# Decoder layer on one core: the down projection in two column passes, with every third chunk of two row tiles as seven block products

## The chip, the cores and the metric

The kernel runs on one core of one Trainium2 chip. The metric is the time of one execution on the device in microseconds (us), as the median of several runs. The core has five engines that run their own queues in order: TensorE (PE, with PEld for the loading of its stationary operand), VectorE (DVE), ScalarE (ACT), GpSimd (POOL) and SyncE (SP, which here only issues DMA transfers).

## The reference, cut to what matters

One decoder layer, 256 tokens of 2048 features: a combined projection, two kinds of attention, an output projection and a layer norm, and then the part that the change is about:

```python
def conv_ffn(h, w_up, conv_w, conv_b, w_down):
    u = h @ w_up
    g, val = u[..., :FFN_DIM], u[..., FFN_DIM:]
    ...
    gc = conv_b + sum(conv_w[j] * gp[:, j:j + S] for j in range(CONV_W))
    return (jax.nn.silu(gc) * val) @ w_down
...
f = conv_ffn(h, w_up[l], conv_w[l], conv_b[l], w_down[l])
h = layer_norm(DEEPNORM_ALPHA * h + f, ln2_g[l], ln2_b[l])
```

FFN_DIM is 5632, so the down projection multiplies [256 tokens, 5632] by [5632, 2048], all float32.

## The kernel before, in words

**Products in three parts.** TensorE is fed float32r operands. Each float32 operand is split into hi (rounded by a ScalarE copy) and lo (the VectorE difference between the operand and hi), and a product is the sum of hi\*hi, hi\*lo and lo\*hi. So each weight chunk costs ScalarE one pass (L122, in `split`) and VectorE one pass (L123), each in two halves of 128x1024; each tile of activations costs one pass of 128x256 on either engine (L447 and L448, in `split_act`).

**A stream of chunks.** All weights come as one stream of chunks of 1 MB, [128 rows, 2048 columns], the raw chunks in 4 buffers (`raws`) and the hi and lo halves in 6 buffers each (`splits`). A step of the program works off one chunk. The order of the instructions on every engine is the order in which the program is written out; nothing reorders it. At the start of step i, `begin(i)` issues what runs ahead: the split of the activations of chunk i+2, the second half of the split of chunk i+2, the DMA of chunk i+6 on SP, and then whatever an earlier step left to be done now (`at`, `pending`). Halfway through, `middle(i)` issues the first half of the split of chunk i+3. As the engines work their queues in order, an instruction that waits for a buffer holds back all that was issued after it on its engine.

**The down projection.** There are 44 chunks of 128 of the 5632 features (FT = 44), each with all 2048 output columns. The eight PSUM banks hold the whole result, [128 tokens, 512 columns] for 2 token halves t and 4 column groups c. In step i, `mm_d` (through `mm_token`) issues for each of the eight banks the three products with 512 moving columns, 24 in all, through the one line L190. Column groups 0 and 1 come first, then `middle(i)`, then 2 and 3. So the first half of a chunk's hi and lo buffers is free at midstep, which is what `split` of chunk i+3 waits for.

**The tail.** The last four chunks (PAIRED_END = 4) are taken bank by bank, so that the first token half is complete early; the layer norm of that half (`z_piece` L381 and L384, `ln_stats`, `finish_pool` L770 to L772 on ACT and POOL) runs beside the products of the second half. Two of the four chunks are kept in buffers of their own (`ends`). The residual and the result are in `z`, [128, 2, 2048].

Of the kernel before, what the change touches and what calls it, by code (L numbers as in the profile page):

```python
# [11 lines left out]
F32 = mybir.dt.float32  # L12
# [4 lines left out]
P = 128  # L17
D = 2048
S = 256
# [16 lines left out]
# columns of the pack of per-partition vectors  # L36
# [5 lines left out]
PAIRED_END = 4  # L42


@with_exitstack
def hymba_layer(ctx: ExitStack, tc: tile.TileContext, a: dict):
# [16 lines left out]
    # ------------------------------------------------------------ weights  # L63
# [12 lines left out]
    for f in range(FT):  # L76
        # the first two hold g and val of the first 128 features together, half of the rows each
        stream.append(("g", f, 0, a["w_u"][f, 0]))
        stream.append(("u", f, 0, a["w_u"][f, 1]))
    for f in range(FT):  # L80
        stream.append(("d", f, 0, a["w_d"][f]))
# [5 lines left out]
    def pieces(i, half=None):  # L87
        """Column ranges in which a chunk is loaded (or one half of it split): short where all else waits for it."""
# [9 lines left out]
    def load(i):  # L98
        if i >= NS:
            return  # L100
        t = raws.tile([P, 2048], F32, name="raw")
        for x, y in pieces(i):
# [5 lines left out]
    def split(i, half, both=None):  # L108
        """hi and lo parts of half a chunk's columns, in the rotating buffers or in both."""
# [16 lines left out]
    def weights(i, x, w):  # L126
        """hi and lo parts of columns x to x + w of chunk i."""
# [3 lines left out]
    # ------------------------------------------------------------ activations of the layer's input  # L131
    # hi and lo parts of a row tile side by side, so that one product takes both
# [13 lines left out]
    # ------------------------------------------------------------ constants  # L146
# [24 lines left out]
    def lambdas():  # L171
# [8 lines left out]
        # -lambda = (exp(l2) - exp(l1)) - lambda_init  # L180
# [7 lines left out]
    # ------------------------------------------------------------ matrix products  # L188
# [3 lines left out]
    def mm_feature(dst, i, t2):  # L192
        """dst, a bank: [128 features, 256 tokens] twice, to be added up; the weights stand still."""
# [7 lines left out]
    def added(dst, src):  # L201
        """dst = the sum of a bank's two halves."""
# [3 lines left out]
    def mm_token(dst, i, x, ah, al, first, last):  # L206
        """dst, banks of [128 tokens, 512 features], from the chunk's columns x and on; the tokens stand still."""
# [8 lines left out]
    # ------------------------------------------------------------ attention  # L216
# [103 lines left out]
    def mixed(h, scale):  # L320
        """hi and lo parts of a head's output, [head dim, tokens]."""
# [46 lines left out]
    # ------------------------------------------------------------ layer norm  # L368
# [96 lines left out]
    def begin(i):  # L465
# [3 lines left out]
        if j < NS and stream[j][0] == "d":  # L469
            split_act(stream[j][1])  # L470
# [422 lines left out]
```

## Time and profile before

| | |
|---|---|
| median of 3 runs | 1147.85 us (1146.7 to 1148.57) |
| profiled execution, span from first to last instruction | 1146.0 us |
| mean granted TensorE clock in it | 0.997 |
| PE busy, share of the span | 1132.2 us, 99% |
| PEld busy | 967.8 us, 84% |
| DVE busy | 747.7 us, 65% |
| ACT busy | 570.1 us, 50% |
| POOL busy | 20.8 us, 2% |
| read from HBM | 214.80 MB, 189 GB/s over the span |

The time of the profiled execution is given as its span; it lies 1.85 us below the median of the runs. Times in the profile are microseconds unless marked ns. A row of instruction groups gives line, engine, operation, output<-inputs with shapes and count, then busy time and the mean of one in ns, then the idle time of the engine ahead of them and what ended it. Matmuls overlap in the profile: one of 512 columns shows some 390 ns, but the next starts well before that has passed, so the rate is read from starts, not from durations.

### The profile page before, as it was taken

The page shows a single profiled execution, that of the slowest core. Times are in us where ns is not written, and L with a number is a line of the kernel's source. Part 1 is how long each engine was busy: PE and PEld are TensorE (multiplying, and loading weights), DVE is VectorE, ACT ScalarE, POOL GpSimd, SP SyncE. Part 2 cuts the span into 40 slices and gives each one's busy share as a digit, 9 for nine tenths or more (in the row PEclk, how much of TensorE's full clock was granted, in tenths as well). Part 3 has the DMA queues.
Part 4 walks back from the last instruction along what each step waited for, and adds up shares of the span by engine and source line. Part 5 has one row for each costly group of instructions (what it writes and reads, how often), then busy time and mean ns, then how long its engine had stood idle before and what let it go on. Part 6 is the DMA issues. An engine that isn't in the chain of part 4 may idle for free.

```text
span 1146.0 us, 15269 instructions
## 1 busy us (share of the span) xinstructions
PE 1132.2 (99%) x5992; PEld 967.8 (84%) x5992; DVE 747.7 (65%) x1183; ACT 570.1 (50%) x895; POOL 20.8 (2%) x27
## 2 busy tenths in 40 slices
PE   9999999999999999999999999999999999999996
PEld 6888888888888898888888888888888888888885
DVE  6895886857745777777656666566666555555566
ACT  6555554544443485454554545455454444444441
POOL 0000000000000000000000000000000000000004
PEclk9999999999999999999999999999999999999998
DMA  9765455455455456555555555555555555556521
GB/s 329 280 220 193 153 179 179 154 182 184 156 178 190 174 219 222 184 187 190 194 201 185 184 188 187 200 193 188 184 184 193 195 192 191 184 210 233 185 106 74
DMA packets 33768, 217.89 MB, mean 190 GB/s; under 512 B 3744, under 2 KB 5664, under 8 KB 8480
## 3 DMA queue, kind: packets, MB, share of 16 engines
q1 hardware_dynamic: 33696, 216.92, 53.2%
q8 instruction: 47, 0.77, 0.3%
q14 instruction: 25, 0.20, 0.1%
HBM read 214.80 MB, written 2.10 MB: 189 GB/s over the span
## 4 chain that ended last, share of the span: by engine, by line
PE 98%; DVE 1%; POOL 1%; DMA 0%; ACT 0%; issue 0%; SPq 0%; POOLq 0%
PE bank L190 97%; PE bank L313 0%; POOL z L772 0%; DMA raw<-in_w_v 0%; POOL z L771 0%; DVE z L780 0%; PE bank L595 0%; PE bank L360 0%; ACT hf L598 0%; DVE h L610 0%; POOL rstd L392 0%; DVE z L822 0%; DVE bank L821 0%; DVE st L384 0%; DVE z L776 0%
## 5 line engine op out<-in xcount | busy, mean ns | idle before, releaser
L123 DVE TENSOR_TENSOR lo<-raw,hi 128x1024 fp32r<-128x1024 f32 (+1 forms) x394 | 468.0, 1202 | 283.8 <-ACT hi L122 283.4
L122 ACT ACTIVATE hi<-raw 128x1024 fp32r<-128x1024 f32 (+1 forms) x394 | 404.3, 1038 | 282.5 <-PE bank L190 252.4
L190 PE MATMUL bank<-h,hi 128*128 128x512 f32 x1376 | 477.2, 390 | 0.0
L190 PE MATMUL bank<-h,lo 128*128 128x256 f32 x1376 | 388.0, 282 | 0.0
L190 PEld LDWEIGHTS bank<-h,hi 128*128 128x128 f32 x1376 | 258.2, 188 | 54.1
L190 PEld LDWEIGHTS bank<-h,lo 128*128 128x128 f32 x1376 | 260.1, 189 | 0.0
L190 PE MATMUL bank<-x,hi 128*128 128x512 f32 x512 | 181.6, 396 | 0.0
L190 PE MATMUL bank<-x,lo 128*128 128x256 f32 x512 | 144.3, 282 | 0.0
L190 PEld LDWEIGHTS bank<-x,hi 128*128 128x128 f32 x512 | 96.1, 188 | 21.7 <-issue 1.3
L190 PE MATMUL bank<-hi,al 128*128 128x512 f32 (+1 forms) x338 | 107.1, 393 | 0.0
L190 PE MATMUL bank<-lo,ah 128*128 128x512 f32 (+1 forms) x338 | 107.1, 393 | 0.0
L190 PE MATMUL bank<-hi,ah 128*128 128x512 f32 (+1 forms) x338 | 107.1, 393 | 0.0
L190 PEld LDWEIGHTS bank<-x,lo 128*128 128x128 f32 x512 | 96.8, 189 | 0.2
L190 PE MATMUL bank<-hi,x 128*128 128x512 f32 x256 | 86.3, 407 | 0.4 <-ACT hi L122 0.4
L190 PEld LDWEIGHTS bank<-hi,al 128*128 128x128 f32 x338 | 63.7, 188 | 14.7
L190 PEld LDWEIGHTS bank<-lo,ah 128*128 128x128 f32 x338 | 63.7, 188 | 14.7
L190 PEld LDWEIGHTS bank<-hi,ah 128*128 128x128 f32 x338 | 63.6, 188 | 14.7
L190 PEld LDWEIGHTS bank<-hi,x 128*128 128x128 f32 x256 | 49.1, 192 | 13.0 <-ACT hi L122 1.3
L427 ACT ACTIVATE gc<-gs,vec 128x256 f32<-128x256 f32 x43 | 25.9, 602 | 58.7 <-DVE gs L204 58.7
L190 PE MATMUL bank<-lo,x 128*128 128x512 f32 x128 | 51.5, 402 | 0.0
L430 ACT ACTIVATE gc<-gc 128x256 f32<-128x256 f32 x44 | 18.4, 418 | 48.9 <-DVE gc L429 48.9
L447 ACT ACTIVATE ah<-act 128x256 fp32r<-128x256 f32 x44 | 18.2, 416 | 49.2 <-DVE lo L123 45.5
(122 smaller groups left out, 828.7 us busy)
## 6 DMA issues: line engine op xcount, KB each, us to landing
raw<-in_w_u SPq DMA_DIRECT2D x88, 1024.0 KB, 4.8
raw<-in_w_d SPq DMA_DIRECT2D x44, 1024.0 KB, 4.8
raw<-in_w_qk SPq DMA_DIRECT2D x32, 1024.0 KB, 4.9
raw<-in_w_o SPq DMA_DIRECT2D x16, 1024.0 KB, 4.8
raw<-in_w_v SPq DMA_DIRECT2D x12, 1024.0 KB, 4.8
raw<-in_w_v SPq DMA_DIRECT2D x8, 256.0 KB, 4.8
raw<-in_w_v SPq DMA_DIRECT2D x4, 512.0 KB, 7.9
z<-in_x SPq DMA_DIRECT2D x1, 2048.0 KB, 9.7
```

Source lines behind the costliest of these rows:

```text
L122: ACT.activation(hi[:, s], t[:, x:y], AF.Copy)
L123: DVE.tensor_tensor(lo[:, s], t[:, x:y], hi[:, s].bitcast(F32), ALU.subtract)
L190: PE.matmul(out, lhsT, rhs, start=start, stop=stop)
L427: ACT.activation(gc, g, AF.Identity, bias=vec[:, C_CB + f:C_CB + f + 1], scale=w[2])
L430: ACT.activation(gc, gc, AF.Silu)
L447: ACT.activation(hi, src, AF.Copy)
```

## The change

The down projection is done in two passes n over the output columns, 1024 columns each. A step now takes two row tiles of the weights (features 2p and 2p+1, 256 features) and half of the columns: still 1 MB and, in an ordinary step, still 24 products; 22 steps in each pass. PT is FT // 2 = 22 in the diff. Four banks (CB) accumulate the pass's result, and the other four (MB) hold four of the seven products described next.

In every third step (p = 2, 5, ..., 20 in the first pass and 1, 4, ..., 16 in the second: 13 steps) the 2 by 2 blocks of tokens by features, and of features by columns, are multiplied with seven block products in the form of Strassen and Winograd instead of eight: 21 instructions instead of 24. For this, four sums of activation blocks (`act_sums`, VectorE, 128x128 each) and four sums of weight blocks (VectorE, 128x512 each) are formed and split into hi and lo. Three of the seven weight operands are plain blocks: their hi is a ScalarE copy of 1536 columns, and their lo is made by a ScalarE copy with scale -1 into the place of lo, to which a DMA issued on POOL's queue adds the raw blocks (`accum_op`). All seven operands lie in one buffer (`slot`), of which there is one. The four shared products are added into `z` once per pass by `shared_out` (one ScalarE copy, eight VectorE operations), one step after the pass's last seven-product step.

At the end of the first pass, the four CB banks are added into `z` by `z_piece` in the midst and at the end of that step, and the second pass starts over in the same banks. The tail is as before, with pairs of row tiles: the last four steps of the second pass, for the 1024 columns that it holds. Each chunk is loaded by two DMAs instead of one, in rows of 2 KB and 4 KB instead of 8 KB.

```diff
+SEVEN = (range(2, PT, 3), range(1, PT - PAIRED_END, 3))
-    for f in range(FT):
-        stream.append(("d", f, 0, a["w_d"][f]))
+    for n in range(2):
+        for p in range(PT):
+            stream.append(("d", p, n, None))
...
+            src = [a["w_d"][2 * p + k][:, n * 1024:(n + 1) * 1024].rearrange("p (b c) -> p b c", c=512) for k in range(2)]
+            SP.dma_start(b[:, 0:4:3], src[0])
+            SP.dma_start(b[:, 1:3], src[1])
...
+        if k == 0 and late < 3:
+            return (work.tile([P, S], F32R, name="ah", tag="e0", bufs=3),
+                    work.tile([P, S], F32R, name="al", tag="e1", bufs=3))
+        if late < 1:
+            return work.tile([P, S], F32R, name="bh", tag="pt"), work.tile([P, S], F32R, name="bl", tag="on")
...
+    def act_sums(i):
...
+        f = [keep.tile([P, 2, P], F32, name="sf", tag=g) for g in ("cos_d", "sin_d")]
+        DVE.tensor_tensor(f[0][:, 0], a21, a11, ALU.subtract)
+        DVE.tensor_tensor(f[0][:, 1], a22, a21, ALU.subtract)
+        DVE.tensor_tensor(f[1][:, 0], f[0][:, 1], a11, ALU.add)
+        DVE.tensor_tensor(f[1][:, 1], a12, f[1][:, 0], ALU.subtract)
+    def act_sums_split(i):
...
+        for j in range(2):
...
+            ACT.activation(hi, f[j], AF.Copy)
+            DVE.tensor_tensor(lo, f[j], hi.bitcast(F32), ALU.subtract)
+    def blocks_raw(i):
...
+        slot = keep.tile([P, 2, 7, 512], F32R, name="slot", tag="t2")
+        ACT.activation(slot[:, 1, 0:3], t[:, 0:3], AF.Copy, scale=-1.0)
+        POOL.dma_start(slot[:, 1, 0:3], t[:, 0:3], accum_op=ALU.add)
+        f = [work.tile([P, 512], F32, name="tf", tag="m1") for _ in range(2)]
+        DVE.tensor_tensor(f[0], t[:, 0], t[:, 3], ALU.subtract)
+        DVE.tensor_tensor(f[1], t[:, 3], t[:, 2], ALU.add)
...
+        for j in range(2):
+            ACT.activation(slot[:, 0, 3 + j], f[j], AF.Copy)
+        ACT.activation(slot[:, 0, 0:3], t[:, 0:3], AF.Copy)
+    def blocks_lo(i):
...
+        for j in range(2):
+            DVE.tensor_tensor(slot[:, 1, 3 + j], f[j], slot[:, 0, 3 + j].bitcast(F32), ALU.subtract)
+    def blocks_sum(i, j):
...
+        DVE.tensor_tensor(f[0], t[:, 2 - j], f[0], ALU.subtract)
+        ACT.activation(slot[:, 0, 5 + j], f[0], AF.Copy)
+        DVE.tensor_tensor(slot[:, 1, 5 + j], f[0], slot[:, 0, 5 + j].bitcast(F32), ALU.subtract)
...
     def begin(i):
...
         j = i + 2
+        split_act(j - 1, 1)
+        split_act(j, 0)
+        if j < NS and seven(j):
+            blocks_raw(j)
+        else:
+            split(j, 1)
+        if j - 1 < NS and seven(j - 1):
+            blocks_sum(j - 1, 1)
+            act_sums_split(j - 1)
         load(i + 6)
         pending(i)
     def middle(i):
...
+        if i + 2 < NS and seven(i + 2):
+            blocks_lo(i + 2)
+            act_sums(i + 2)
+            blocks_sum(i + 2, 0)
+        if i + 3 < NS and not seven(i + 3):
             split(i + 3, 0)
...
+    def mm_seven(i):
...
+        for m, lhs, b in ((5, s1, 3), (7, s3, 4), (6, s2, 5), (1, a11, 0), (2, a12, 1), (3, s4, 2), (4, a22, 6)):
...
+            if m == 6:
+                middle(i)
+            mm_three(key, dst, lhs, (slot[:, 0, b], slot[:, 1, b]))
+    def shared_out(n):
...
+        ACT.activation(u, MB[1], AF.Copy)
+        z_add(n, 0, 0, u, ALPHA)
+        DVE.tensor_tensor(u, MB[6], u, ALU.add)
+        z_add(n, 0, 1, MB[5], ALPHA)
+        z_add(n, 0, 1, u)
+        DVE.tensor_tensor(u, MB[7], u, ALU.add)
+        z_add(n, 1, 1, MB[5], ALPHA)
+        z_add(n, 1, 0, u, ALPHA)
+        z_add(n, 1, 1, u)
...
+        if i == last[0] - 2:
+            split(last[3], 0, end1)
+            split(last[3], 1, end1)
+        if i == last[0] - 1:
+            split(last[2], 0, end0)
+            split(last[2], 1, end0)
+            for j in last[1:]:
+                for k in range(2):
+                    split_act(j, k)
+        if seven(i):
+            mm_seven(i)
+            if p == SEVEN[n][-1]:
+                at(i + 1, shared_out, n)
+        else:
+            for k in range(2):
+                mm_d(i, 0, [0, 1], k)
+            if n == 0 and p == PT - 1:
+                for c in range(2):
+                    z_piece(0, c, CB[0][c], 2, alpha=1.0)
+            if i < last[0] - 1:
+                middle(i)
+            for k in range(2):
+                mm_d(i, 1, [0, 1], k)
+            if n == 0 and p == PT - 1:
+                for c in range(4):
+                    z_piece(1, c, CB[1][c // 2][:, c % 2 * 256:c % 2 * 256 + 256], 2, 256, 1.0)
```

Of the activations' hi and lo, the second tile of a pair (`bh`, `bl`) has two buffers, the first tile's have three (a pool's tag has the number of buffers that the pool was made with, two in `work`, where a tile names no other). In the last seven-product step's successor, `shared_out` stands in the queues ahead of the splits of `end0` and of the last five activation tiles.

168 lines of the change are left out of this document (111 added, 57 removed).

## The prediction

> **What bounds the kernel now.** I read the page first: engine shares and the chain that ended last.
>
> ```profile
> span 1146.0 us, 15269 instructions
> PE 1132.2 (99%) x5992; PEld 967.8 (84%) x5992; DVE 747.7 (65%) x1183; ACT 570.1 (50%) x895; POOL 20.8 (2%) x27
> PE 98%; DVE 1%; POOL 1%; DMA 0%; ACT 0%; issue 0%; SPq 0%; POOLq 0%
> ```
>
> TensorE ends everything; the rest waits for it. A product taken away is worth its whole slot, as long as what feeds TensorE stays ahead. Next the down projection by itself, as a table of stretches (columns: us, then busy us of each engine, clock, DMA share, GB/s), and two copies of an activation tile, 37 steps apart, in order of time:
>
> ```profile
> 950.00:1000.00 50.00, 50.00 (x217) 40.54 (x216) 25.69 (x28) 22.86 (x27) 0.00 (x0) 1.00 0.53 187
> 894.36 0.42 ACT L447 ACTIVATE ah<-act 128x256 fp32r<-128x256 f32 x1 [1.27 <-PE bank L190]
> 1100.71 0.42 ACT L447 ACTIVATE ah<-act 128x256 fp32r<-128x256 f32 x1 [1.27 <-DVE lo L123]
> ```
>
> TensorE has no gap, VectorE is half busy (25.69 of 50), ScalarE 22.86. A step lasts (1100.71 - 894.36)/37 = 5.577 us, a product 5.577/24 = 0.2324 us. VectorE and ScalarE wait, and for what the list of waits says:
>
> ```profile
> DVE lo L123 <- ACT hi L122: 283.4, 263, 2.2
> ACT hi L122 <- PE bank L190: 252.4, 165, 2.4
> ```
>
> ScalarE waits for TensorE to free a buffer, VectorE for ScalarE: slack, but in a serial chain. That is the view to carry into the change.
>
> **What the change removes.** 13 steps have 21 products instead of 24: 39 x 0.2324 = **-9.06 us**. The order of TensorE's instructions bears the count out: 51 fewer of 512 columns, 24 more of 256 in the tail, 51 - 12 = 39.
>
> **What it adds: durations.** From the groups by shape (third number: ns of one):
>
> ```profile
> L123 DVE TENSOR_TENSOR lo<-raw,hi 128x1024 fp32r<-128x1024 f32 x378 | 456.9, 1223 | 278.0 <-ACT hi L122 277.7
> L123 DVE TENSOR_TENSOR lo<-raw,hi 128x512 fp32r<-128x512 f32 x16 | 11.0, 690 | 5.8 <-ACT hi L122 5.7
> L448 DVE TENSOR_TENSOR al<-act,ah 128x256 fp32r<-128x256 f32 x44 | 18.6, 425 | 21.0 <-PE bank L190 20.9
> L303 DVE TENSOR_SCALAR e<-e,rs 128x128 f32<-128x128 f32 x8 | 2.3, 287 | 0.3
> L122 ACT ACTIVATE hi<-raw 128x1024 fp32r<-128x1024 f32 x378 | 394.3, 1056 | 275.9 <-PE bank L190 252.4 <-issue 19.1 <-DMA raw<-in_w_qk 2.6
> L122 ACT ACTIVATE hi<-raw 128x512 fp32r<-128x512 f32 x16 | 10.1, 628 | 6.5 <-DMA raw<-in_w_v 6.3
> L447 ACT ACTIVATE ah<-act 128x256 fp32r<-128x256 f32 x44 | 18.2, 416 | 49.2 <-DVE lo L123 45.5 <-PE bank L190 3.7
> L190 PEld LDWEIGHTS bank<-hi,ah 128*128 128x128 f32 x338 | 63.6, 188 | 14.7
> L203 ACT ACTIVATE us<-bank 128x256 f32<-128x256 f32 x43 | 15.5, 360 | 0.0
> L204 DVE TENSOR_TENSOR us<-bank,us 128x256 f32<-128x256 f32 x43 | 18.0, 418 | 0.0
> ```
>
> A ScalarE copy of 1536 columns is not there; from 512 to 1024 it grows by 428, so 1484. VectorE sums of 128 columns: 290. Handovers, in order of time:
>
> ```profile
> 891.83 0.64 PE L190 MATMUL bank<-hi,ah 128*128 128x512 f32 x2
> 892.03 1.06 ACT L122 ACTIVATE hi<-raw 128x1024 fp32r<-128x1024 f32 x1 [1.13 <-PE bank L190]
> 1095.60 1.06 ACT L122 ACTIVATE hi<-raw 128x1024 fp32r<-128x1024 f32 x1
> 1096.69 1.23 DVE L123 TENSOR_TENSOR lo<-raw,hi 128x1024 fp32r<-128x1024 f32 x1 [0.60 <-ACT hi L122]
> 1131.08 0.41 DVE L381 SCALAR_TENSOR_TENSOR z<-z,bank 128x256 f32<-128x256 f32 x1
> 1131.52 0.43 DVE L384 BATCH_NORM_STATS2 st<-z 128x6 f32<-128x256 f32 x1
> 1131.87 0.40 DVE L381 SCALAR_TENSOR_TENSOR z<-z,bank 128x256 f32<-128x256 f32 x1
> ```
>
> TensorE to ScalarE takes about 0.19 after the next product begins, ScalarE to VectorE 0.03 (1096.66 to 1096.69). On one engine an independent instruction begins some 0.06 before its forerunner's end, a dependent one 0.02 after (0.79 for a pair of 0.405 and 0.428). A stationary operand that TensorE waits for costs its load too, 0.19 + 0.03.
>
> **One group of three steps (N, N, seven).** `begin` of the first N is held at its very start: the second activation tile has two buffers and `slot` one, both freed by the last product of the seven-step before. From there (time 0), in queue order, start to end:
>
> ```
> ACT  two act hi 0.19-0.96 | neg 0.90-2.39 | f0,f1 hi 2.33-3.52 | hi 3.46-4.95 | sum hi 5.89-6.51 |
>      split 6.45-7.51 | two act 7.45-8.22 | split 8.16-9.22 | sum hi 11.32-11.94 | sh 11.88-12.30, 12.24-12.66
> DVE  two act lo 0.64-1.43 | f0,f1 1.37-2.69 | lo,lo 2.99-4.31 | four sums 4.25-5.23 | sum 5.17-5.86 |
>      lo 6.54-7.23 | split 7.54-8.76 | two act 8.70-9.49 | split 9.43-10.66 | sum 10.60-11.29 |
>      lo 11.97-12.66 | sl 12.60-13.03, 12.97-13.39
> PE   N 0-5.58 | N 5.58-11.16 | seven: first product needs sh, its third needs sl
> ```
>
> The first product starts at 12.30 + 0.22 = 12.52 instead of 11.16 (1.36 late), the third at 13.03 + 0.22 = 13.25 instead of 12.98 (0.27). So each seven-step loses 1.63 and wins 3 x 0.2324 = 0.70: a net loss of 0.93. Twelve steps like this: **+19.6**. The first of all has the last gate and value tiles (one ScalarE copy of some 0.36, two VectorE passes of 0.42) ahead of it in the queues: another 0.5. With no overlap between instructions the loss is 2.53 a step, +30.4; that is the upper bound. The lower bound is nothing: a chain shorter by 1.4.
>
> **The DMA on POOL's queue.** No row shows an adding DMA or one issued by POOL. Issued at 2.39, it is needed by the tenth product, 13.25 + 0.23 + 6 x 0.2324 = 14.9 at the earliest: 12.5 us to land 768 KB. Nearest rows (KB, us to landing):
>
> ```profile
> raw<-in_w_d SPq DMA_DIRECT2D x44, 1024.0 KB, 4.8
> z<-in_x SPq DMA_DIRECT2D x1, 2048.0 KB, 9.7
> out<-z SPq DMA_DIRECT2D x1, 768.0 KB, 3.3
> ```
>
> From 3.3 (the same size) to 14.4 (three times 1 MB, for two reads and a write beside the loads). I take it as hidden, nearest to the row of its own size; the far end costs (14.4 - 12.5) x 13 = 25 us. The Trainium skill, DMA: Bandwidth & Descriptors, section Anatomy of one DMA, puts a DMA from this queue at 2.0 us plus bytes over 436 GB/s, an estimate of 3.8 us here: hidden, nothing to add. POOL's queue has nothing else then. On SP, the raw buffer of a seven-chunk goes free only after its last sum, at 11.29, and the loads of the next two chunks wait behind that; the first of them is split in the next group, at 17.7 + 6.45, so 12.8 us are there for the 4.8 of the row of in_w_d. The split of each load in two, the smaller rows and the freed buffers I cost at nothing for that reason.
>
> **Between the passes.** Step 21 of the first pass begins as a group does, but `shared_out` and the `z_piece`s stand on VectorE ahead of the group's remaining work:
>
> ```profile
> L381 DVE SCALAR_TENSOR_TENSOR z<-z,bank 128x512 f32<-128x512 f32 x12 | 8.2, 684 | 9.0 <-PE bank L190 9.0
> L384 DVE BATCH_NORM_STATS2 st<-z 128x6 f32<-128x512 f32 x12 | 8.3, 695 | 0.4
> L381 DVE SCALAR_TENSOR_TENSOR z<-z,bank 128x256 f32<-128x256 f32 x8 | 3.2, 405 | 0.0
> L384 DVE BATCH_NORM_STATS2 st<-z 128x6 f32<-128x256 f32 x8 | 3.4, 428 | 0.3
> L234 ACT ACTIVATE val<-bank 128x512 f32<-128x512 f32 x4 | 2.3, 583 | 0.0
> ```
>
> ScalarE's copy of the bank (0.59) ends at 5.47. VectorE: eight of `shared_out` 5.50-10.87; two `z_piece` pairs 10.81-13.55, the second bank free at 12.84; the group's lo, sums and split, with their ScalarE partners, 13.49-19.27; four `z_piece` pairs of 256 columns 19.21-22.44, the last bank free at 21.99; then the rest, sh at 25.98. TensorE enters the second pass at 12.87 instead of 5.58 (**7.29**), its second half at 22.02 instead of 15.65 (**6.37**), the seven-step at 26.20 instead of 24.81 and with its 0.27 (**1.65**): **+15.3**. Without overlap it is 17.0; the lower bound is again nothing, if VectorE were through in time.
>
> **The tail.** After the last seven-step (0) VectorE still has a split, three more and two activation tiles, until 4.51; then `shared_out` to 9.83, two splits of `end0` to 12.15, and the second tile of chunk 19 at 12.52. TensorE is through step 17 at 5.58 and needs that tile's lo after 11 more products, at 8.13, and gets it at 12.52 + 0.22: **+4.6** (5.7 without overlap; nothing at the least). From there 48 + 48 products' worth as before; the half that ends first hands over to POOL as before, so all that follows moves by as much.
>
> **Sum**: -9.06 + 19.6 + 0.5 + 15.3 + 4.6 = +30.9, against the profiled 1146.0: 1176.9. The median of the runs lies 1.85 higher; 1147.85 + 30.9 = **1178.8 us**.
>
> **Rivals.**
> (1) *The group's chain is shorter than my sums* and the seven-steps wait for nothing, while the two ends stay: -9.06 + 13.7 + 4.6 = +9.2, 1157. For it: VectorE has only 25.69 of 50 us busy. Against: the chain's length is serial, not load.
> (2) *TensorE's gaps make it slow again.* At the start, TensorE is at half rate:
>
> ```profile
> 7.39 0.63 PE L190 MATMUL bank<-lo,x 128*128 128x512 f32 x1
> 7.82 1.05 PE L190 MATMUL bank<-hi,x 128*128 128x512 f32 x2
> 9.98 0.63 PE L190 MATMUL bank<-hi,x 128*128 128x512 f32 x2
> 10.45 0.40 PE L190 MATMUL bank<-lo,x 128*128 128x512 f32 x1
> 5.00:10.00 5.00, 4.78 (x12) 3.49 (x13) 3.25 (x7) 3.17 (x8) 0.00 (x0) 1.00 1.01 342
> ```
>
> 0.43 a product at 7.4, 0.235 at 10, though the clock column says 1.00. If gaps of 4.6 us and more bring that back for twelve products, each costs 12 x 0.2 = 2.4: after the 7.29 covered by the wait that follows, after the 6.37 covered but for 1.0 (24.81 + 2.4 against 26.20), after the 4.6 in full: 1.0 + 2.4 = +3.4, 1182.2. The Trainium skill, TensorE: Matmul & The Clock Gate, Part 1, has the half rate return after an idle window of about 3.4 us; by that rule all three gaps would, the 1.4 ones not. No row here shows a gap in mid-kernel.
> (3) *The adding DMA lands late*: +25, 1204.
> (4) *Not slower*: the only mechanism that gets there is VectorE keeping up everywhere. It decides where all its waits together, 40.0 by my sum, fall below the 9.06 won. The place is the entry to the second pass: the banks would have to be free at 5.58, where ten VectorE instructions of some 0.69 stand behind a ScalarE copy that ends at 5.47. Without any wait it is -9.06: 1138.8. Only much shorter instructions than in the rows would do it. That the products are not saved is excluded by the count.
>
> **How the numbers follow.** The forecast 0.62, (1) 0.13, (2) 0.12, (3) 0.08, (4) 0.05. The forecast's own width is from 1168 (stalls of 0.75 a step) to 1192 (no overlap: -9.06 + 30.4 + 0.5 + 17.0 + 5.7 = +44.5). The range 1156 to 1197 takes in (1) and (2) and leaves out (3) and (4). Differences under 0.2% (2.3 us) can't be told from none by a measurement of this kernel: faster 0.04, same 0.01, slower 0.95.
>
> **What would show it.** TensorE idle about 1.6 us ahead of and in each seven-step, put down to ScalarE's `sh` (the copy in `act_sums_split`) and VectorE; 7 and 6 us around the entry to the second pass, put down to VectorE; 4 to 5 us in the tail; VectorE's instructions from `begin` starting at the end of a seven-step. Wrong: seven-steps that follow without a gap, a wait for the DMA's buffer `slot`, or gaps after which products start 0.43 apart.

## The result, and the profile after

The changed kernel takes **1179.09 us** (median of 4 runs, 1178.41 to 1179.91); the kernel before took 1148.05 (4 runs). The ratio is 1.0275, with a 95% interval of 1.026 to 1.0289. The forecast was 1178.8. The profiled execution has a span of 1177.1 us, 31.1 more than before. From the page of the changed kernel: the span, the engines' busy times, the granted TensorE clock in 40 slices, and the engines' shares of the chain that ended last.

```profile
span 1177.1 us, 15646 instructions
PE 1136.3 (97%) x5965; PEld 962.7 (82%) x5965; DVE 822.5 (70%) x1399; ACT 622.7 (53%) x1019; POOL 32.0 (3%) x40
PEclk9999999999999999999999999999999999889988
PE 87%; DVE 6%; issue 2%; ACT 2%; DMA 1%; SPq 0%; POOL 0%; ACTq 0%; DVEq 0%
```

27 matmuls fewer are there (51 of 512 columns less, 24 of 256 more), yet TensorE is busy 4.1 us longer, and it holds 87% of the chain instead of 98. The clock line shows where the longer busy time comes from: in the down projection, the last quarter, it has 8 in place of 9 (the last 8 also covers the end, where TensorE has nothing left to do). The share of the chain went to waits. The list of waits of the same kernel (us in total, times, the longest) names the releasers:

```profile
PE bank L206 <- DVE z L397: 9.6, 4, 5.4
PE bank L206 <- ACT sh L504: 9.6, 12, 1.7
PEld bank L206 <- DVE sl L505: 5.5, 12, 0.5
PE bank L206 <- DVE eh L480: 6.2, 1, 6.2
```

Before, TensorE waited in this stage for nothing. Where each wait stands, in order of time: TensorE's first matmuls of the stage in the kernel before and in the changed one (the first two rows), then the matmuls of the changed kernel with an idle time ahead (in brackets, with the releaser). The row of 937.23 stands for eleven.

```profile
889.05 0.62 PE L190 MATMUL bank<-hi,ah 128*128 128x512 f32 x2
```

```profile
888.33 0.62 PE L206 MATMUL bank<-hi,ah 128*128 128x512 f32 x2
901.26 0.73 PE L206 MATMUL bank<-slot,sh 128*128 128x512 f32 x2 [1.72 <-ACT sh L504]
902.61 1.05 PE L206 MATMUL bank<-slot,sh 128*128 128x512 f32 x2
...
937.23 0.73 PE L206 MATMUL bank<-slot,sh 128*128 128x512 f32 x2 [0.72 <-ACT sh L504]
...
1022.47 0.76 PE L206 MATMUL bank<-hi,ah 128*128 128x512 f32 x1 [5.37 <-DVE z L397]
...
1137.86 0.50 PE L206 MATMUL bank<-hi,eh 128*128 128x512 f32 x1 [1.01 <-ACT eh L479]
1144.82 0.79 PE L206 MATMUL bank<-hi,eh 128*128 128x512 f32 x1 [6.23 <-DVE eh L480]
```

The table of stretches of the changed kernel gives the same by engine (us; busy us of PE, PEld, DVE, ACT, POOL; granted clock; DMA share; GB/s): a first group of three steps, a regular one, and the one around the change of pass. Below it are the issues of the adding DMA, one after each seven-step, on both sides of the change of pass.

```profile
901.26:920.01 18.75, 18.00 (x70) 13.96 (x70) 13.58 (x25) 11.43 (x19) 0.88 (x1) 0.91 0.72 210
937.23:954.46 17.23, 16.49 (x69) 12.81 (x70) 13.58 (x25) 11.43 (x19) 0.86 (x1) 1.00 0.77 226
1006.13:1037.50 31.37, 21.72 (x69) 15.97 (x70) 25.05 (x47) 12.75 (x21) 0.87 (x1) 0.80 0.44 132
```

```profile
1013.83 0.87 POOL L517 DMA_DIRECT2D slot<-raw  x1 [16.34 <-ACT slot L516]
1045.35 0.87 POOL L517 DMA_DIRECT2D slot<-raw  x1 [30.64 <-ACT slot L516]
```

A regular group takes 17.225 us ((1006.13 - 920.01)/5 = 17.224). Three steps of before are 16.73, and with three products less a group should take 16.03: it loses 1.19, of which 0.72 stand in the bracket and 0.46 (5.5/12) are weight loads waiting for `sl`. The books, against the kernel before:

| part | forecast | measured | how |
|---|---|---|---|
| 39 products | -9.06 | -9.06 | counts |
| 11 regular seven-steps | +17.9 | +13.1 | 11 x 1.19 |
| the first one | +2.1 | +3.7 | waits 2.2 (the 1.19 of the others, and 1.0 more ahead: 1.72 for 0.72), then 8 products at 0.43, 1.5 |
| change of pass | +15.3 | +15.5 | 1045.35 - 1013.83 = 31.52 instead of 16.03 |
| tail | +4.6 | +9.06 | idle 1.01 + 6.23, the operands' loads behind it 0.4, then 7 products at 0.43, 1.4 |
| ahead of the stage, and after the last column of the first 128 tokens is in z | 0 | -1.2 | 888.33 for 889.05; 1177.1 - 1155.03 = 22.07 for 1146.0 - 1123.44 = 22.56 |
| sum | +30.9 | +31.1 | spans 1177.1 and 1146.0 |

The earlier start of the stage, in the last row but one, is chance: in the runs below, whose programs are the same up to there, it begins between 887.9 and 889.8. So the total was right, and two terms were off by 4.8 and 4.5 us, in opposite directions. The experiments ask for the causes of each term.

### The profile page after: what moved, and what is told of

The parts are those of the page before. It is cut to its first block, busy times and chain, and to the rows that moved or that the text cites. A ratio compares the mean times of both kernels' runs of the same rounds, so it can differ in the third digit from the quotient of the medians.

```text
span 1177.1 us, 15646 instructions
## 1 busy us (share of the span) xinstructions
PE 1136.3 (97%) x5965; PEld 962.7 (82%) x5965; DVE 822.5 (70%) x1399; ACT 622.7 (53%) x1019; POOL 32.0 (3%) x40
## 4 chain that ended last, share of the span: by engine, by line
PE 87%; DVE 6%; issue 2%; ACT 2%; DMA 1%; SPq 0%; POOL 0%; ACTq 0%; DVEq 0%
PE bank L206 87%; DVE lo L139 2%; ACT hi L138 1%; DVE tf L535 1%; DVE z L861 1%; DMA raw<-in_w_d 1%; DVE bl L480 0%; PE bank L329 0%; DVE al L480 0%; DMA raw<-in_w_v 0%; ACT sh L504 0%; DVE end L139 0%; DVE st L400 0%; DVE z L397 0%; DVE slot L529 0%
## 5 line engine op out<-in xcount | busy, mean ns | idle before, releaser
L139 DVE TENSOR_TENSOR lo<-raw,hi 128x1024 fp32r<-128x1024 f32 (+1 forms) x368 | 436.0, 1200 | 206.8 <-ACT hi L138 206.3
L138 ACT ACTIVATE hi<-raw 128x1024 fp32r<-128x1024 f32 (+1 forms) x368 | 375.9, 1034 | 214.6 <-PE bank L206 187.0
L206 PE MATMUL bank<-hi,ah 128*128 128x512 f32 (+1 forms) x118 | 39.2, 404 | 9.6 <-DVE z L397 9.6
L536 ACT ACTIVATE slot<-tf 128x512 fp32r<-128x512 f32 x26 | 16.4, 632 | 55.1 <-DVE tf L535 55.1
L206 PE MATMUL bank<-slot,sh 128*128 128x512 f32 x104 | 35.0, 419 | 9.6 <-ACT sh L504 9.6
L206 PE MATMUL bank<-hi,mh 128*128 128x512 f32 x128 | 42.1, 400 | 0.0
L206 PE MATMUL bank<-lo,mh 128*128 128x512 f32 x128 | 41.6, 395 | 0.0
L206 PE MATMUL bank<-hi,ml 128*128 128x512 f32 x128 | 41.6, 395 | 0.0
L444 DVE SCALAR_TENSOR_TENSOR gc<-gs,vec,gc 128x255 f32<-128x255 f32 x43 | 20.8, 484 | 28.8 <-ACT gc L443 28.8
```

The source lines that it names most:

```text
L138: ACT.activation(hi[:, s], t[:, x:y], AF.Copy)
L139: DVE.tensor_tensor(lo[:, s], t[:, x:y], hi[:, s].bitcast(F32), ALU.subtract)
L206: PE.matmul(out, lhsT, rhs, start=start, stop=stop)
L444: DVE.scalar_tensor_tensor(gc[:, 1:], g[:, 0:S - 1], w[1], gc[:, 1:], op0=ALU.mult, op1=ALU.add)
L536: ACT.activation(slot[:, 0, 5 + j], f[0], AF.Copy)
```

## Experiments

Theory: TensorE waits for what VectorE and ScalarE make for a seven-step, by the **order** in which their queues hold it, and it waits most where a seven-step stands beside other VectorE work (the change of pass, the tail). Rivals: the column passes cost by themselves; the adding DMA or the weight loads bound; TensorE's half rate after gaps is the loss.

### 1. Column passes without seven-steps

```
-SEVEN = (range(2, PT, 3), range(1, PT - PAIRED_END, 3))
+SEVEN = (range(0), range(0))
```

(and the residual's scale back in `z_piece`, since `shared_out` doesn't run.)

> The two column passes alone: every chunk by eight products, no block sums, the stored streams and their residual scaling in the two passes as in the changed kernel. First theory: the whole loss belongs to the seven-steps (their stalls, the waits for VectorE at the change of pass that only stand there because the last seven-step's sums are still being taken out of the banks, the tail). Then this kernel is within 3 us of the kernel before, 1148 to 1151 us, and its profile has no wait of more than about 2 us at the change of pass. Rival: the column passes themselves cost, by half-width rows of the weights and by the bank hand-over between passes; then most of the 15.5 us at the change of pass stays and the time is 1160 us or more.

Measured: 1148.16 us, ratio 1.0004 (0.9995 to 1.0014). All of TensorE's waits for other engines in this stage, from the list of waits of this run:

```profile
PEld bank L206 <- DVE z L397: 1.9, 2, 1.4
PE bank L206 <- DVE z L397: 1.3, 2, 1.1
```

Half-width rows, twice as many loads and the hand-over of the banks together cost 0.4 us, which the interval does not tell from nothing. The rival is out: the passes lose 15 us only beside a seven-step.

### 2. Which products go first

```
-for m, lhs, b in ((5, s1, 3), (7, s3, 4), (6, s2, 5), (1, a11, 0), (2, a12, 1), (3, s4, 2), (4, a22, 6)):
+for m, lhs, b in ((1, a11, 0), (2, a12, 1), (5, s1, 3), (7, s3, 4), (6, s2, 5), (3, s4, 2), (4, a22, 6)):
```

> The changed kernel with the products of a seven-step in another order: the two that need no sum of activations or of weights come first, the ones whose left factor is the last split of ScalarE come behind them. Nothing is computed differently. First theory: the 1.2 us that each regular seven-step loses and the 1.8 us gap ahead of the first one are waits for the split of the sums on ScalarE, and two products (6 matmuls, some 2.8 us) ahead of them cover the whole wait; 11 x 1.19 + 3.7 = 16.8 us less at most, 1162 to 1165 us, with no stop on the split of sums left in the list of waits. Rival: the seven-steps are slow for what they load beside it (the adding DMA, the copies) and the wait only shows it; then the wait moves to another releaser with the same length and the time stays at 1177 to 1181 us.

Measured: 1167.12 us, ratio 1.0171 (1.0154 to 1.0188); 12 us less than the changed kernel, 2 short of the theory. A regular and an irregular group in the table of stretches of this run, and TensorE in the irregular one:

```profile
939.77:955.71 15.94, 15.94 (x71) 12.92 (x70) 13.57 (x25) 11.44 (x19) 0.86 (x1) 1.00 0.82 244
1081.95:1101.77 19.82, 17.80 (x71) 14.02 (x70) 13.56 (x25) 11.43 (x19) 0.87 (x1) 0.91 1.00 342
```

```profile
1093.02 0.51 PE L206 MATMUL bank<-slot,ah 128*128 128x512 f32 x1 [2.02 <-DMA slot<-raw]
```

A regular group has no gap left (15.94 busy of 15.94): the stall was the wait for the split. The six matmuls put ahead take 6 x 0.2324 = 1.4 us, not the 2.8 of the expectation, and that is enough. But the first product now reads what the adding DMA writes, and once, in a stretch where the DMA engines were busy all the time, that DMA came 11.1 us after its issue at 1081.95; the wait and the half rate behind it cost 19.82 - 15.94 = 3.9 us. The prediction's rival of a late DMA had a place after all, in another order of the products.

### 3. The tail: the last sums later

```
+            shared_out(1)          # at step last[0] - 1, behind split_act
         if seven(i):
             mm_seven(i)
-            if p == SEVEN[n][-1]:
+            if p == SEVEN[n][-1] and n == 0:
```

> The changed kernel with one move in the tail: the sums of the last seven-step that VectorE adds into z are taken behind the splits and the activation tiles of the final steps, not ahead of them. First theory: the 6.2 us stop of TensorE before the final products is VectorE working off those sums before it makes the last low parts; without them 4 to 6 us go, 1173 to 1175 us, and the 4 us wait of ScalarE for the last weight load stays. Rival: the stop is that late load, whatever VectorE does ahead of it; then the time stays within 2 us of the changed kernel, 1177 to 1181 us.

Measured: 1172.97 us, ratio 1.0219 (1.0204 to 1.0235): 6.1 us less, at the lower edge of the theory. ScalarE's wait for the load is still there, TensorE's gaps behind it are short (same view of this run):

```profile
1129.98 2.02 ACT L138 ACTIVATE end<-raw 128x1024 fp32r<-128x1024 f32 x2 [3.90 <-DMA raw<-in_w_d]
```

```profile
1136.77 0.50 PE L206 MATMUL bank<-hi,eh 128*128 128x512 f32 x1 [0.37 <-ACT eh L479]
1139.04 0.50 PE L206 MATMUL bank<-hi,eh 128*128 128x512 f32 x1 [1.53 <-DVE eh L480]
```

The place of the sums is a cause of the tail. That does not yet clear the load, which held up both engines for 4 us ahead of them (experiment 11).

### 4. No seven-step beside the change of pass and the tail

```
-SEVEN = (range(2, PT, 3), range(1, PT - PAIRED_END, 3))
+SEVEN = (range(2, PT - 3, 3), range(1, PT - PAIRED_END - 2, 3))
```

> The changed kernel with two seven-steps fewer (11 in place of 13): the last one before the change of pass and the last one before the tail are ordinary steps again. 6 products of 0.232 us come back (+1.4 us). First theory: the 15.5 us at the change of pass and the 9 us of the tail are the price of where these two stand, since the sums of a seven-step next to a border queue on VectorE with the border's own work; with ordinary steps there some 8 us of the one and 8 us of the other go and two stalls of 1.2 us: 1162 to 1166 us. Rival: the borders are dear for any neighbour, as the passes are; then two seven-steps fewer give back only their stalls, 2.4 us less and 1.4 us more, 1177 to 1180 us.

Measured: 1159.94 us, ratio 1.0111 (1.0096 to 1.0126). TensorE's gaps around the change of pass and in the tail:

```profile
1021.14 0.50 PE L206 MATMUL bank<-hi,ah 128*128 128x512 f32 x1 [3.90 <-DVE z L397]
1022.70 0.80 PE L206 MATMUL bank<-hi,ah 128*128 128x512 f32 x1 [1.07 <-DVE z L397]
...
1126.45 0.50 PE L206 MATMUL bank<-hi,eh 128*128 128x512 f32 x1 [0.92 <-DVE eh L480]
```

19.2 us less for two seven-steps fewer, 2 more than expected: both borders give back about 8 us. Of the rest, 1.5 us are the half rate behind the first gap, which has the same 1.7 us here and is followed by products at 0.23 (the first group takes 17.22 instead of 18.75; experiment 8, and the rows at the very end). What is left at the change of pass, 3.9 and 1.1 us, is VectorE preparing the first seven-step of the second pass ahead of the last four `z_piece` pairs.

### 5. Two products ahead, without what the DMA writes

```
+first, lo_last = ((0, 0), (1, 0)), ((0, 1),)      # (act part, weight part)
+every = ((0, 0), (0, 1), (1, 0))
+for m, lhs, b, xy in ((1, a11, 0, first), (2, a12, 1, first), (5, s1, 3, every), (7, s3, 4, every),
+                      (1, a11, 0, lo_last), (2, a12, 1, lo_last), (6, s2, 5, every), ...
```

> The order of the run with two products ahead, and in it the two matmuls that read the low parts which the adding DMA writes come after the fifth and seventh product, not first. Nothing is computed differently. In that run a seven-step group takes 15.95 us, three steps less the product saved, but one group of the second pass takes 19.8 because a matmul waits 2.0 us for that DMA. First theory: this wait is the whole rest, and with some 4 us more of lead it is gone: 1167.1 - 3.9 = 1163 us, 1162 to 1165, with no wait on the DMA. Rival: the queue that carries the weights has no room left in the second pass at the higher pace, so a later need only shifts which transfer is late; then a wait on a weight load takes its place and the time stays at 1166 to 1169 us.

Measured: 1168.47 us, ratio 1.0185 (1.0168 to 1.0202). The time is in the rival's range, but no load is waited for, and neither is the DMA. The weight loads' waits in this run:

```profile
PEld bank L206 <- DVE sl L505: 5.5, 12, 0.5
PEld bank L206 <- ACT sh L504: 3.5, 12, 1.2
```

Neither expectation holds as written. Only four matmuls (0.93 us) stand ahead now instead of six (1.4), which covers less than the 1.19: the DMA is issued every 16.30 us instead of every 15.95, 0.35 us a group, over eleven groups 3.9 us, as much as the DMA's wait had cost. The 1.4 us by which this run is slower than experiment 2 are not explained by that.

### 6. Experiments 4 and 5 together

> The same order, with the 11 seven-steps that stay clear of the last step before the change of pass and of the tail. Theory: the two edits add, since they take away different waits: the run with 11 seven-steps had 1159.9 us, its ten regular groups lose 17.22 - 15.95 = 1.27 us each and its first some 3.4 more, so 1159.9 - 12.7 - 3.4 = 1143.8, 1142 to 1146 us, faster than the kernel before. Its wait of 3.9 us at the change of pass stays, since VectorE still makes the sums of the second pass's first seven-step there. Rival: a TensorE that comes earlier finds VectorE and the loads less far ahead; the stalls come back at the borders, and it ends at 1147 us or more.

Measured: 1151.32 us, ratio 1.0035 (1.0022 to 1.0048), a miss for the theory. The sum of the expectation took a group at 15.95 us; with the 16.30 of experiment 5 it is 1159.9 - 9 x 0.92 - 0.9 = 1150.7. The gaps at the borders are those of experiment 4 (3.90, 0.77 and 0.91 us), so the rival's reason doesn't apply, though its time does.

### 7. The second pass's seven-steps one step later

```
-SEVEN = (range(2, PT, 3), range(1, PT - PAIRED_END, 3))
+SEVEN = (range(2, PT - 3, 3), range(2, PT - PAIRED_END - 2, 3))
```

(with the order of experiment 5)

> As the run with 11 seven-steps and the new order, with those of the second pass one step later (steps 2, 5, 8, 11, 14 in place of 1, 4, 7, 10, 13), so that VectorE has no sums of a seven-step to make while it takes the first pass's results out of the banks. Theory: what remains at the change of pass is what the column passes alone had there, waits of 0.2 and 1.1 us, in place of 3.9 and 1.1 us with 4 us of products at half rate behind them: 4 to 5 us less, 1139 to 1142 us, near the 1148.2 - 33 x 0.232 = 1140.5 us that the saved products allow. Rival: the work of VectorE is only shifted and the first seven-step of the pass then waits for its sums; then it stays at 1143 to 1146 us.

Measured: 1149.69 us, ratio 1.0015 (1.0006 to 1.0025). A miss for the theory: 1.6 us less than experiment 6, not 4 to 5.

```profile
1011.35 0.47 PE L206 MATMUL bank<-hi,ah 128*128 128x512 f32 x1 [0.22 <-DVE z L397]
1014.65 0.51 PE L206 MATMUL bank<-hi,ah 128*128 128x512 f32 x1 [0.28 <-DVE z L397]
1026.27 0.96 PE L206 MATMUL bank<-slot,sh 128*128 128x512 f32 x2 [2.37 <-ACT sh L504]
```

The change of pass is as short as with the passes alone, but the wait has moved to the first seven-step behind it, as the rival said: its split of the sums comes 2.4 us late, and some eight products run at half rate behind that.

### 8. From what gap the half rate comes

On experiment 1, in 18 steps; `mm` writes a bank that nobody reads then.

```
+    def gap(widths):
+        mm(MB[1], idle[:, 0:P], idle, True, True)
+        DVE.tensor_copy(idle[:, 0:P], MB[1][:, 0:P])
+        for w in widths:
+            POOL.tensor_tensor(idle[:, 0:w], idle[:, 0:w], idle[:, 0:w], ALU.add)
+        mm(MB[1], idle[:, 0:P], idle, True, True)
```

> The column passes alone, without seven-steps, and in 18 steps a wait of graded length put into TensorE: a small matmul, a copy by VectorE, none to six operations of GpSimd on the copy, and a small matmul that needs the last of them. What is added feeds nothing. It asks from which length of a wait the products behind it run at 0.43 us in place of 0.23. First theory: there is a bound between the 0.72 us that never brought it and the 1.72 us that did, and behind every longer wait the slow products last some 4 us, whatever the wait's length, so each wait costs its length and about 2 us. Rival: the slow stretch grows with the wait, so that short ones cost little beyond their length. Second rival: the wait's length has nothing to do with it (the slow products in the changed kernel come from the operands of the seven-step), and none of the 18 brings them below the 3.4 us that the page "TensorE: Matmul & The Clock Gate" of the Trainium skill gives in Part 1 for the idle window.

Measured: one run, 1267.79 us. The gaps came out between 2.15 and 11.67 us. Two of them, each by the matmul that ends it, and then the table of stretches around it (us; busy us of PE, PEld, DVE, ACT, POOL; granted clock; DMA share; GB/s), cut into stretches of 3.41 us:

```profile
937.12 0.39 PE L206 MATMUL bank<-idle 128*128 128x512 bf16 x1 [2.74 <-POOL idle L912]
934.99:938.40 3.41, 1.28 (x6) 1.09 (x7) 3.35 (x5) 1.58 (x4) 0.51 (x1) 1.00 0.64 239
938.40:941.81 3.41, 3.41 (x10) 2.63 (x9) 0.08 (x1) 0.00 (x0) 0.00 (x0) 0.50 0.55 148
...
1032.20 0.39 PE L206 MATMUL bank<-idle 128*128 128x512 bf16 x1 [3.38 <-POOL idle L912]
1027.15:1030.56 3.41, 1.67 (x8) 0.95 (x6) 1.07 (x1) 2.16 (x4) 0.00 (x0) 1.00 0.59 166
1030.56:1033.97 3.41, 1.77 (x8) 1.48 (x9) 3.00 (x5) 0.45 (x1) 1.15 (x1) 1.00 0.36 144
1033.97:1037.38 3.41, 3.41 (x17) 2.76 (x16) 0.00 (x0) 0.00 (x0) 0.00 (x0) 1.00 0.67 185
```

| gap, us | products behind it |
|---|---|
| 2.15, 2.58, 2.85, 3.06, 3.38 | full rate |
| 2.74, 2.95, 3.17, 3.27 | half rate, mostly after about 1 us at full rate |
| 3.92 to 11.67 (nine gaps) | half rate, from the first one on |

No bound by length separates these: 2.74 brings it, 3.38 doesn't. The first theory falls, and so does the second rival, since four gaps under 3.4 us do bring it. The rival of a stretch that grows with the gap falls too: once the products start again, half rate is left for 3.2 us after 3.92, for 3.4 after 11.67, and for 5.4 at the most.

What separates them is in the column of the granted clock. In all these traces, up to the stretch in which TensorE's work ends, it stands at 0.50 only for 3.41, 6.83 or 10.24 us at a time, once, twice or three times 3.41, and within a run all of these begin on one grid of 3.41 us. Cut on that grid, the gap of 2.74 leaves TensorE busy for 1.28 of 3.41 us, idle for 0.62 of them, and the next 3.41 us are at half clock. The gap of 3.38, though longer, falls on two stretches, each idle for about half (0.51 and 0.48), and none follows at half clock. Over the 18 gaps, the stretch that was idle most was idle for 0.61 or more of its length where half rate came and for 0.51 or less where it did not. In the changed kernel the gap ahead of the first seven-step lies within one stretch:

```profile
898.54:901.95 3.41, 1.69 (x7) 0.79 (x5) 2.71 (x5) 1.68 (x4) 0.00 (x0) 1.00 0.32 70
901.95:905.36 3.41, 3.39 (x9) 2.67 (x9) 3.21 (x6) 2.07 (x4) 0.00 (x0) 0.50 0.93 342
```

So the bound is on the idle share of a window of 3.41 us, and lies near one half: in all runs of this case, with the clock full before, 0.46 and less never brought half rate, 0.59 and more always did, and from 0.47 to 0.51 both happened (the ends of matmuls are modelled, so the shares are not exact). Two short gaps in one window add up: at the change of pass of this run, waits of 0.53 and 1.06 us brought half rate from 1061.28 on. Where a gap falls on the grid is chance, and that decides for single gaps of 1.7 to 3.4 us. (At the start of the kernel before, where the prediction found half rate beside a clock of 1.00, the trace has no record of the clock ahead of 9.49 us.) The Trainium skill, TensorE: Matmul & The Clock Gate, Part 1, describes a free-running window of about 3.4 us; the trace agrees, with its grid of 3.41, while its "after ≥1 idle window" does not agree with the four short gaps above, where a window was idle for 0.61 to 0.76 of its length only.

### 9. The split of the sums ahead of the seventh weight sum

```
 if j - 1 < NS and seven(j - 1):
-    blocks_sum(j - 1, 1)
     act_sums_split(j - 1)
+    blocks_sum(j - 1, 1)
```

> The changed kernel, all 13 seven-steps, products in its own order; two calls change places: in the step before a seven-step the split of the activation sums stands ahead of the seventh weight sum, not behind it. First theory: the 1.19 us stall is the place of that split in ScalarE's queue. ScalarE stood idle for 2.14 us there, for a weight sum of VectorE that is needed five products later; ahead of it the split is done some 2.7 us sooner, which covers the 1.19 of the regular steps and the 1.7 us gap of the first. 11 x 1.19 + 3.7 = 16.8 us less, 1161 to 1164 us, groups of 15.95 to 16.05 us, no late DMA since its need is where it was. Rival: VectorE is the bound of the chain, and what is put behind moves the wait to the seventh weight sum or to the low parts; then a group stays above 16.5 us and the time above 1170.

Measured: 1164.44 us, ratio 1.0148 (1.0133 to 1.0164). ScalarE in a step ahead of a seven-step, first in the changed kernel, then here:

```profile
953.47 0.63 ACT L536 ACTIVATE slot<-tf 128x512 fp32r<-128x512 f32 x1 [2.14 <-DVE tf L535]
954.01 0.71 ACT L504 ACTIVATE sh<-sf 128x256 fp32r<-128x256 f32 x2
```

```profile
946.02 0.71 ACT L504 ACTIVATE sh<-sf 128x256 fp32r<-128x256 f32 x2
...
948.92 0.63 ACT L536 ACTIVATE slot<-tf 128x512 fp32r<-128x512 f32 x1 [2.20 <-DVE tf L535]
```

The split no longer stands behind a 2.1 us wait for an operand that is needed five products later, and groups take 15.95 us, as in experiment 2, but with the products that read what the DMA writes at their old place. 14.7 of the 16.8 us come: the seven-step ahead of the change of pass gains nothing, since there VectorE sets the end (31.44 us between the DMA issues around it, 31.52 in the changed kernel), and the tail gives some 0.9 back. So the stall of a regular group is two calls in the wrong order, not a lack of VectorE's or ScalarE's time.

### 10. Eleven seven-steps, later ones in the second pass, split first

The `SEVEN` of experiment 7, the edit of experiment 9, products in the changed kernel's order.

> The 11 seven-steps at 2, 5, 8, 11, 14, 17 of the first pass and 2, 5, 8, 11, 14 of the second, with the split of the activation sums ahead of the seventh weight sum, products in the changed kernel's order. Theory: in the run with these steps and four products put ahead (1149.7 us) what was left were 0.35 us in each of 9 regular groups, 0.8 at the first step, and a gap of 2.4 us with some 2 us of half rate behind it at the first seven-step of the second pass, all on the split; without them 1149.7 - 3.2 - 0.8 - 4.4 = 1141.3, 1140 to 1143 us, faster than the kernel before by about 0.55%, near the 1148.2 - 33 x 0.232 = 1140.5 that the saved products allow. Rival: at full pace the loads or the adding DMA come late, as in one group of the run with two products ahead; then a wait on a DMA appears and it ends between 1143 and 1149 us.

Measured: **1142.35 us** (5 runs, 1141.39 to 1143.93) against 1147.39, ratio 0.9958 (0.9945 to 0.997): faster than both kernels. A stretch of 50 us in the middle of the stage, and TensorE at the first seven-step behind the change of pass:

```profile
950.00:1000.00 50.00, 50.00 (x218) 40.66 (x217) 44.11 (x73) 33.45 (x53) 1.72 (x2) 1.00 0.80 249
```

```profile
1020.21 0.73 PE L206 MATMUL bank<-slot,sh 128*128 128x512 f32 x2 [0.55 <-ACT sh L504]
1021.75 0.50 PE L206 MATMUL bank<-slot,sl 128*128 128x512 f32 x1 [0.81 <-DVE sl L505]
```

TensorE has no gap in these 50 us although VectorE is busy 44.1 of them, where the kernel before had 25.7. 33 products less are worth 7.7 us, of which 5.0 to 5.8 are kept (against the kernel before, and against experiment 1). The first seven-step of the second pass waits 0.55 and 0.81 us where it waited 2.37, and behind no gap of this stage the products are at half rate. TensorE waits for no DMA for more than 0.5 us; ScalarE waits for weight loads once for 1.25 and, in the tail, once for 2.5 us, so the rival's late loads are there but cost TensorE little (its only gap there is 0.9 us, put down to VectorE).

### 11. The tail: the last load split later

```
-        if i == last[0] - 2:
-            end1 = keep.tile([P, 4, 1024], F32R, name="end1", tag="mb")
-            split(last[3], 0, end1)
-            split(last[3], 1, end1)
         if i == last[0] - 1:
             ...                       # end0 and the activation tiles
+            end1 = keep.tile([P, 4, 1024], F32R, name="end1", tag="mb")
+            split(last[3], 0, end1)
+            split(last[3], 1, end1)
```

> The changed kernel with one move in the tail: the splits of the last weight load stand one step later, behind the splits of the load before it and of the activation tiles, so that ScalarE no longer stops for that load with work queued behind it; the sums of the last seven-step stay where they are. First theory: the 4.05 us that ScalarE stands still there hold up everything queued behind on both engines, and that is what the tail costs beyond the 4.6 us of the prediction; without them the 6.2 us gap of TensorE shrinks by about 4 and 1 to 2 us of half rate go: 1173 to 1175.5 us. Rival: the sums of the seven-step on VectorE are the whole tail (without them it lost 6.1 us less, with the wait for the load still there), and the load costs nothing of its own; then it stays at 1177.5 to 1180 us.

Measured: 1173.76 us, ratio 1.0228 (1.0214 to 1.0242): 5.3 us less, within the theory. The same split of the last load on ScalarE, first in the changed kernel, then here, with TensorE's one gap left in this tail:

```profile
1130.59 2.02 ACT L138 ACTIVATE end<-raw 128x1024 fp32r<-128x1024 f32 x2 [4.05 <-DMA raw<-in_w_d]
```

```profile
1134.10 2.00 ACT L138 ACTIVATE end<-raw 128x1024 fp32r<-128x1024 f32 x2
```

```profile
1139.37 0.50 PE L206 MATMUL bank<-hi,eh 128*128 128x512 f32 x1 [2.52 <-DVE eh L480]
```

The total is within the theory, but not all of it is the tail. In the two profiles, from the last seven-step to the last column of the first 128 tokens, the tail takes 26.52 us for 31.26, 4.7 less: the idle time shrinks, and the half rate stays (8 products, 1.5 us), though the theory had it go. The rest is chance: 1.5 us less because the first seven-step's gap brings no half rate here, and 1.2 more because the stage begins later. Without the stop the tail costs 9.06 - 4.7, about 4.3 us, near the 4.6 of the prediction, though a third of it is half rate, which the forecast had left out. Either edit takes away half of the tail or more, since the final low parts come after both: 4 us of waiting for a load and 5.3 us of sums, of which TensorE's lead covers only part.

## Why the prediction was right, and where its steps were not

- **The products.** -9.06 as counted.
- **The stall of a regular seven-step.** The mechanism was right: the split of the sums sets the first product, the low parts the third, and experiments 2 and 9 remove exactly that. Its size was off: 1.19 us instead of 1.63, in part because instructions on one engine overlap more than the 0.06 us taken (two copies of 256 columns are through in 0.71, row of 954.01, for 0.78 in the prediction): the split begins 11.50 us after the group's first product at 942.51, where the working had 11.88. And the first product follows it after 0.45 us (954.46) instead of 0.64, since the load of its operand holds it up less than the 0.22 taken. Over eleven steps 4.8 us too much.
- **The first seven-step.** 3.7 instead of 2.1. The waits are 2.2, as in the working (1.63 + 0.5); what was missing is the half rate behind them, 1.5.
- **The adding DMA.** Hidden, as forecast: a median of 6.5 us to landing in the row below (10.2 at the most), against the 12.5 that were there. The estimate of 3.8 us from the Trainium skill, DMA: Bandwidth & Descriptors, Anatomy of one DMA, is short of the trace, which decides.

```profile
slot<-raw POOLq DMA_DIRECT2D x13, 768.0 KB, 6.5
```

- **The change of pass.** 15.5 for 15.3, with the waits put down to the cause that was worked out: VectorE's queue holds `shared_out`, the `z_piece`s and the next seven-step's preparation in that order. Experiments 1, 4 and 7 take its neighbours away one by one: 1.3 us of idle with no seven-step near, 5.0 with only the later one, 0.5 with none in the step behind. Half rate runs behind these gaps (clock 0.80 in the stretch), and not all of it is under a wait: the seven-step's third product starts at 1038.51, while its low part is there from about 1037.4 on (VectorE begins it at 1036.93). So the waits come to some 14.4 us, less than forecast, and about 1.1 of half rate, which the second rival had (1.0) and the forecast had not, makes up for it.
- **The tail.** 9.06 for 4.6. The step that failed reads "The split of each load in two, the smaller rows and the freed buffers I cost at nothing". For a regular group that holds: by the working the next split of a load is 12.8 us away, and no load is waited for there. In the tail the step ahead of the last splits `end1`, the last load of all, which had stood on SP behind the load that waited for the seven-chunk's buffer; ScalarE stopped 4.05 us for it with all the tail's work queued behind. Experiment 11 shows the price, 4.7 us. The half rate of 1.4 us behind the gap, which the second rival had (2.4), stays there; in experiment 3, whose gaps are 0.37 and 1.53 us, it is gone.
- **The rivals.** (1), a chain that is shorter, holds for a quarter of the stall, not for all of it. (2) happened, and beyond its rule: 1.5 us at the first seven-step after a gap of only 1.7, some 1.1 at the change of pass and 1.4 in the tail, together 4.0 for the 3.4 it gave. (3) did not happen in this order of the products, and once, for 3.9 us, in that of experiment 2. (4), VectorE keeping up everywhere, was excluded with reason for this kernel; experiment 10 gets there, not by shorter instructions but by another place for the steps and another order of two calls.

So the forecast met the time within 0.3 us with a term 4.8 too high, two terms 4.5 and 1.6 too low, and 1.2 outside the stage that no term had; half rate, 4.0 us in all, was in none of its terms. The mechanism of the waits was right; that the sum is so close is chance.

## What to carry to other kernels

Where an engine with slack feeds the one that bounds, look at the order in its queue before its load: a wait for a late operand ahead of an early one costs the bounding engine the whole difference, and moving one call was worth 14.7 us here. Keep work that a step adds away from the borders of a stage, where the same engine empties the accumulators: the same seven-steps cost 1.2 us in the middle and 8 us beside a border. And when a step holds a buffer longer, follow the load queue to its end, not only to the next use: the load at the end of the queue has nothing behind it to hide in.

## What the runs showed of the hardware that was not expected

- In mid-kernel the granted clock falls to half for one, two or three stretches of 3.41 us on a grid that runs through the whole execution, after a stretch in which TensorE was idle for about half or more (experiment 8 has the shares). A single gap of 1.53 us or less never brought it here, gaps of 3.9 and more always did, and in between their place on the grid decided. A stretch at half clock takes eight products at 0.427 us, which at full rate take 1.86: some 1.6 us lost. The same gap of 1.72 us ahead of the first seven-step is followed by half rate in the changed kernel (the row of 902.61: 0.85 to the next pair) and by full rate in the run of experiment 11, where it falls on two stretches of the grid:

```profile
902.48 0.73 PE L206 MATMUL bank<-slot,sh 128*128 128x512 f32 x2 [1.72 <-ACT sh L504]
...
903.57 0.63 PE L206 MATMUL bank<-slot,sh 128*128 128x512 f32 x2
```

- The adding DMA takes longer to land at a higher pace of the rest: a median of 6.5 us in the changed kernel with groups of 17.2 us, 7.4 to 7.6 with groups of 16.3 (experiments 5 to 7), and 8.1 to 9.1 with groups of 15.95 (experiments 2, 9 and 10); single ones took up to 11.2.
